# First channel block of a convolution taken in fp32 from the un-normalised input, the norm's factor applied to its sums

## The chip, the cores and the metric

The kernel runs on one core of one Trainium2 chip. The metric is the device time of one execution in microseconds (us). Three executions of the kernel before took 1934.17, 1934.20 and 1934.63 us, median 1934.2 us. A core has a matrix engine (TensorE, in the rows PE, its weight loads PEld), a vector engine (VectorE, DVE), a scalar engine (ScalarE, ACT), a general engine (GpSimd, POOL) and SyncE (SP), which here only issues DMAs. Each works through its own list of instructions in order.

## The reference

The model has two layers on 256 tokens of 2048 channels: a convolution module, an MLP, an attention layer, an MLP. The change touches only the start of the first one.

```python
def rms_norm(x, g):
    xf = x.astype(jnp.float32)
    y = xf * lax.rsqrt(jnp.mean(xf * xf, axis=-1, keepdims=True) + NORM_EPS)
    return (y * g.astype(jnp.float32)).astype(x.dtype)

def conv_module(h, w_pw1, b_pw1, w_dw, b_dw, ln_g, ln_b, w_pw2, b_pw2):
    u = h @ w_pw1 + b_pw1                     # 2048 -> 4096
    a, gate = jnp.split(u, 2, axis=-1)
    u = a * jax.nn.sigmoid(gate)
    u = lax.conv_general_dilated(...) + b_dw  # causal, depthwise, width 31
    u = jax.nn.silu(layer_norm(u, ln_g, ln_b))
    return u @ w_pw2 + b_pw2
...
h = rms_norm(x, norm_mixer_g[layer])
x = x + conv_module(h, ...)
```

## The kernel before

**Products in three parts.** A product of fp32 accuracy is made of three products in the rounded type fp32r: the operand is split into an upper part (`hi`, or the first half of the tile `xt`), rounded by ScalarE, and a remainder (`lo`), subtracted by VectorE or GpSimd. The sum of upper x upper, upper x lower and lower x upper is accumulated in PSUM (`conv_mm`, line 823). A weight half of 128x1024 numbers is rounded at L170 and its remainder made at L174.

**The convolution module.** The first matrix is worked in 16 channel blocks `c` of 128 channels. For each, two accumulators (`va` for the value, `ga` for the gate) take 16 slices `k` of 128 input channels. One block is 16 x 2 x 3 = 96 products of 128x256. The weights of a block come as two loads (`raw`, numbers 2c and 2c+1, two DMAs each, rows of 512 B), each split in two halves of four slices. `glu(c)` makes the gated value `ub` (padded, 256 tokens). Then VectorE adds the 31 taps of the depthwise convolution one instruction at a time (`add_tap`, L910) onto sums that ScalarE starts (`start_sum`, L880); a second sum of the same block ends in the tile `half`, GpSimd adds a side product to it, and L918 joins the two in `ca`. The order of the taps is written out by `dve_taps`: for block c it does most taps, and the last five come mixed with the first ones of block c+1.

**Order.** The whole stage stands under `tc.manual_schedule()`: each engine's order is the order of the code. While TensorE multiplies block c, VectorE adds the taps of block c-1, and ScalarE and GpSimd split the weights of blocks c and c+1.

**The start.** `x` is loaded in six pieces, the first 128 tokens on SP's queue (columns 0-1023, 1024-1535, 1536-2047), the other 128 on ACT's. TensorE turns x slice by slice (`turn0`, L1031) into PSUM, with extra transposes of the identity between (`busy`, L1001) that only keep it occupied. VectorE and ScalarE take sums of squares, and the factor 1/rms (`r0`) is turned into a row over the tokens and copied to `r_row` in the tile `b2`. Then `scaled` multiplies each slice in PSUM by the norm's gain and that row (L1075), `upper` rounds it into `xt` (L1090), `lower` takes the remainder (L1093), and block 0 is multiplied slice by slice as they come. Weight load 0 is asked for behind x on SP's queue. A DMA is issued only when the one eight before it has landed, since eight semaphores are used in turn.

Of the kernel before, what the change touches and what calls it, by code (L numbers as in the profile page):

```python
# [10 lines left out]
F32 = mybir.dt.float32  # L11
# [41 lines left out]
N_WARM = (10, 0, 16, 4)  # L53
# [26 lines left out]
def trunk_kernel(  # L80
# [677 lines left out]
    with ExitStack() as cx:  # L758
# [13 lines left out]
        xn = cv.tile([P, T, D], F32, tag="tok", name="xn")  # L772
        b2 = cv.tile([P, D], F32, name="b2")

        ca = cv.tile([P, KC, S], F32, tag="tok", name="ca")
        sh = cv.tile([P, KC, S], F32R, name="sh")
# [10 lines left out]
        raws, wjs = {}, {}  # L787


        def conv_load(n):  # L790
            if n < NU:
                c, k = n // UC, n % UC * 8
                raws[n] = load(
                    [rows(conv_w_pw1[0], k, 8, c * P, P), rows(conv_w_pw1[0], k, 8, D + c * P, P)], 8,
                    2 if n == 0 else 1,
                )
            elif n < NU + KC // 2:
                raws[n] = load([rows(conv_w_pw2[0], 2 * (n - NU), 2, 0, 2 * NB)], 2)
# [38 lines left out]
        def glu(c):  # L837
            ub = ubs[c] = branches[c % 3]
            sg = cv2.tile([P, S], F32, tag="sg", name=nm("sg"), bufs=1)
            va, ga = pss.pop(c)  # L840
            nc.scalar.activation(sg, ga[:, :S], AF.Sigmoid, bias=b_pw1[:, KC + c : KC + c + 1])
            if c in (0, KC - 2, KC - 1):
# [4 lines left out]
            else:  # L847
                vb = cv2.tile([P, S], F32, tag="vb", name=nm("vb"), bufs=1)
# [138 lines left out]
        for n in range(3):  # L987
            conv_load(n)
# [5 lines left out]
        with tc.manual_schedule():  # L994
# [17 lines left out]
            for i, (c0, c1) in enumerate(X_PARTS[1][:2]):  # L1012
                nc.scalar.activation(xn[:, 1, c0:c1], xs[:, 1, c0:c1], AF.Square, accum_out=xsq[:, i : i + 1])

# [3 lines left out]
            for n in range(NNB - 1):  # L1018
                block_stats(n)

            groups = [[0], [1]] + [[k, k + 1] for k in range(2, 10, 2)] + [[10], [11], [12, 13], [14, 15]]
            where, tiles = {}, {}

            def bank(pt, *ks):
                tiles[ks[0]] = pt
                for i, k in enumerate(ks):
                    where[k] = pt[:, i * S : (i + 1) * S]
# [5 lines left out]
            for k in range(2):  # L1033
                bank(acc_tile() if k else tr_tile(), k, k + 10)
            for k in range(2, 10, 2):
                bank(sum_tile() if k < 6 else sum2_tile() if k == 6 else acc_tile(), k, k + 1)
            for t in range(T):
                turn0(range(8), t)
                busy(N_WARM[t])

            early = [xn[:, 0, :S], b2[:, S : 2 * S]]
            nc.vector.tensor_copy(early[0], where[0])
            block_stats(NNB - 1)
            c0, c1 = X_PARTS[1][2]
            dve_squares(xn[:, 1, c0:c1], xs[:, 1, c0:c1], xsq[:, 2:3])
            for t in range(T):
                turn0(range(8, 11), t)
            pss[0] = [acc_tile()]
            busy(N_WARM[2])
# [9 lines left out]

            for t in range(T):  # L1060
                nc.tensor.transpose(
                    misc[:, t * P : (t + 1) * P], r0[:, t : t + 1].broadcast_to([P, P]), ident
                )
            r_row = b2[:, :S]
            conv_half(0, 0)
            nc.scalar.activation(early[1], where[1], AF.Copy)
            for t in range(T):
                turn0((11,), t)
            pss[0].append(acc_tile())
            for i in range(N_WARM[3]):  # L1070
                nc.tensor.transpose(pss[0][0][:, :P], ident, ident)

            def scaled(*ks):
                for k in ks:
                    nc.vector.scalar_tensor_tensor(  # L1075
# [868 lines left out]
```

## Time and profile before

| | |
|---|---|
| three runs | 1934.17, 1934.20, 1934.63 us (median 1934.2) |
| the profiled execution's own time | 1934.31 us, its span 1932.5 us |
| TensorE busy | 1921.0 us (99%), granted clock 0.999 |
| VectorE busy | 1592.2 us (82%) |
| ScalarE busy | 1095.6 us (57%) |
| GpSimd busy | 249.0 us (13%) |
| DMA | 375.50 MB, mean 194 GB/s |

The 1.8 us between the time and the span lie outside the first and last instruction. Busy time of an engine says how long it held instructions, not whether the kernel waited for it; that is read from the rows of idle time and from the chain of work that ended last. Times in rows are us from the start of the span unless marked ns. A row of the timeline gives start, length, engine, line, operation, the tile written, the tiles read, the count, and in brackets the idle time before it and what ended that. The conv stage before the second matrix is the first 210 us.

### The profile page before, as it was taken

The numbers are of one execution on the slowest core, as the hardware profiler recorded it, in microseconds if no ns is written. First come the engines' busy times: TensorE is split into PE (matmuls) and PEld (weight loads), VectorE is DVE, ScalarE is ACT, GpSimd is POOL, SyncE is SP. The second block draws the span as 40 slices with busy tenths as digits, with TensorE's granted clock in tenths as the row PEclk, the third lists the DMA queues.
The fourth block names the chain that finished last, engine by engine and source line by source line (L and its number), as shares of the span: only waits on it lengthen the run. The fifth ranks groups of instructions, "written<-read, shape, count | busy, mean of one in ns | idle before, by whom it ended". The sixth has DMA issues, their size and how long they took to land.

```text
span 1932.5 us, 28477 instructions
## 1 busy us (share of the span) xinstructions
PE 1921.0 (99%) x10725; PEld 1681.5 (87%) x10725; DVE 1592.2 (82%) x2457; ACT 1095.6 (57%) x1636; POOL 249.0 (13%) x208
## 2 busy tenths in 40 slices
PE   9999999999999999999999999999999999999998
PEld 8999888888888888888898998888888888888887
DVE  7999988877999776799976766877789987678998
ACT  5667755554555545555576655555555554455554
POOL 6999200000010100000001420000000010000000
PEclk9999999999999999999999999999999999999999
DMA  7766456665585866655656545465646776665774
GB/s 230 214 183 189 153 189 206 193 194 177 175 251 194 263 195 187 194 174 196 217 176 175 142 134 192 155 216 186 188 162 225 222 248 212 191 196 175 231 219 150
DMA packets 230427, 375.50 MB, mean 194 GB/s; under 512 B 16392, under 2 KB 107792, under 8 KB 230032
## 3 DMA queue, kind: packets, MB, share of 16 engines
q1 hardware_dynamic: 224640, 363.28, 58.7%
q0 software_dynamic: 4320, 7.87, 2.2%
q10 hardware_dynamic: 1328, 2.52, 0.4%
q8 instruction: 84, 1.38, 0.3%
q14 instruction: 55, 0.45, 0.1%
HBM read 363.68 MB, written 2.10 MB: 189 GB/s over the span
## 4 chain that ended last, share of the span: by engine, by line
PE 97%; DVE 2%; DMA 0%; ACT 0%; issue 0%; ACTq 0%; DVEq 0%
PE acc L655 24%; PE acc L205 15%; PE acc L203 15%; PE acc L204 15%; PE acc L656 13%; PE acc L823 8%; PE acc L1287 2%; DVE sum L910 1%; DMA xs<-in_x 0%; PE acc L1535 0%; PE acc L1566 0%; PE acc L1565 0%; PE acc L1536 0%; PE acc L1564 0%; PE acc L1537 0%; PE tr L267 0%
## 5 line engine op out<-in xcount | busy, mean ns | idle before, releaser
L174 DVE TENSOR_TENSOR lo<-raw,hi 128x1024 fp32r<-128x1024 f32 (+2 forms) x509 | 602.2, 1197 | 232.3 <-ACT hi L170 226.6
L170 ACT ACTIVATE hi<-raw 128x1024 fp32r<-128x1024 f32 (+2 forms) x574 | 583.9, 1036 | 361.1 <-PE acc L655 203.7
L655 PE MATMUL acc<-xt,hi 128*128 128x512 f32 x2048 | 710.6, 390 | 0.0
L656 PE MATMUL acc<-xt,lo 128*128 128x256 f32 x2048 | 577.5, 282 | 0.0
L655 PEld LDWEIGHTS acc<-xt,hi 128*128 128x128 f32 x2048 | 384.3, 188 | 80.7
L656 PEld LDWEIGHTS acc<-xt,lo 128*128 128x128 f32 x2048 | 387.1, 189 | 0.2
L497 ACT ACTIVATE hi<-raw 128x1024 fp32r<-128x1024 f32 x248 | 228.7, 948 | 228.3 <-DVE raw L505 134.0
L498 DVE TENSOR_TENSOR lo<-raw,hi 128x1024 fp32r<-128x1024 f32 x248 | 263.9, 1087 | 27.6 <-ACT hi L497 22.5
L203 PE MATMUL acc<-hi,sh 128*128 128x512 f32 x514 | 200.1, 389 | 0.0
L205 PE MATMUL acc<-lo,sh 128*128 128x512 f32 x514 | 200.1, 389 | 0.0
L203 PE MATMUL acc<-hi,gh 128*128 128x512 f32 (+1 forms) x516 | 200.0, 388 | 0.0
L205 PE MATMUL acc<-lo,gh 128*128 128x512 f32 (+1 forms) x516 | 199.9, 387 | 0.0
L204 PE MATMUL acc<-hi,gl 128*128 128x512 f32 (+1 forms) x516 | 199.9, 387 | 0.0
L823 PE MATMUL acc<-xt,hi 128*128 128x256 f32 x1024 | 180.2, 281 | 0.3 <-ACT b L1106 0.2
L204 PE MATMUL acc<-hi,sl 128*128 128x512 f32 x450 | 175.1, 389 | 0.0
L578 POOL DMA_DIRECT2D xs<-v x30 | 26.5, 994 | 1136.4 <-DVE lo L174 703.2
L910 DVE SCALAR_TENSOR_TENSOR sum<-ub,w_dw,sum 128x256 f32<-128x256 f32 x409 | 164.3, 481 | 3.6 <-ACT sum L880 3.0
L174 POOL TENSOR_TENSOR lo<-raw,hi 128x1024 fp32r<-128x1024 f32 x65 | 155.0, 2410 | 17.3 <-ACT hi L170 17.3
L823 PEld LDWEIGHTS acc<-xt,hi 128*128 128x128 f32 x1024 | 154.8, 188 | 1.1 <-ACT xt L1090 0.6
L823 PE MATMUL acc<-xt,lo 128*128 128x256 f32 x512 | 139.2, 279 | 0.0
L205 PEld LDWEIGHTS acc<-lo,sh 128*128 128x128 f32 x514 | 96.5, 188 | 20.4 <-DVE lo L498 0.3
L204 PEld LDWEIGHTS acc<-hi,gl 128*128 128x128 f32 x516 | 96.9, 188 | 19.9
(314 smaller groups left out, 2531.3 us busy)
## 6 DMA issues: line engine op xcount, KB each, us to landing
raw<-in_mlp_w SPq DMA_DIRECT2D x255, 1024.0 KB, 5.5
raw<-in_conv_w_pw SPq DMA_DIRECT2D x62, 512.0 KB, 5.1
raw<-in_conv_w_pw SPq DMA_DIRECT2D x16, 1024.0 KB, 5.1
raw<-in_mla_w_o SPq DMA_DIRECT2D x16, 1024.0 KB, 5.7
raw<-in_mla_w_kv_up SPq DMA_DIRECT2D x32, 256.0 KB, 3.9
xs<-v POOLq DMA_DIRECT2D x30, 256.0 KB, 7.8
raw<-in_mla_w_in SPq DMA_DIRECT2D x8, 576.0 KB, 3.8
raw<-in_mla_w_in SPq DMA_DIRECT2D x4, 1024.0 KB
```

The costliest lines, as they stand in the source:

```text
L170: nc.scalar.activation(hi, raw[:, js, :], AF.Copy)
L174: eng.tensor_tensor(lo, raw, hi.bitcast(F32), op=ALU.subtract)
L203: nc.tensor.matmul(ps, sh, mh, start=start, stop=False)
L204: nc.tensor.matmul(ps, sl, mh, start=False, stop=False)
L205: nc.tensor.matmul(ps, sh, ml, start=False, stop=stop)
L497: nc.scalar.activation(hi, src, AF.Copy)
L498: nc.vector.tensor_tensor(lo, src, hi.bitcast(F32), op=ALU.subtract)
L655: nc.tensor.matmul(ps[b], wh[:, bs], xhl(k), start=k == 0, stop=False)
L656: nc.tensor.matmul(ps[b][:, :S], wl[:, bs], xh(k), start=False, stop=k == KC - 1)
L823: nc.tensor.matmul(pss[c][b][:, :S], w[i][:, bs], (xh, xl)[j](k), start=k == i + j == 0, stop=end and k == k0 + nk - 1 and (i, j) == terms ...
L910: nc.vector.scalar_tensor_tensor(out=out, in0=ubs[c][:, w : w + S], scalar=tap(c, w), in1=base, op0=ALU.mult, op1=ALU.add)
L1287: nc.tensor.matmul(ps2[b][t], x_kt(k, t), w[:, bs], start=k == g == i == 0, stop=k == KC - 1 and i == len(group) - 1,)
```

## The change

Weight load 0 and x: SP's queue now carries the first two slices of weight load 0 (`first_load(0, 2)`, 256 KB) between the first and the second piece of x, and the rest of it behind x in two steps. `x_load(1, i)`, on ACT's queue, is as before.

Block 0: ScalarE (for three slices VectorE) copies each turned slice times the norm's gain from PSUM to an SBUF tile `xg` (`gained`). `first_products` multiplies the raw fp32 weights with `xg` as plain fp32 products: 32 products of 128x256 in the place of 96 in fp32r. No weight of block 0 is split. The factor 1/rms is multiplied into the two sums of block 0 in `glu(0)` by VectorE, since it depends on the token alone.

For blocks 1 to 15 the normed, split x is still needed: `scaled` multiplies pairs of slices of `xg` by `r_row`, `upper` and `lower` fill `xt` from SBUF, beside the products of block 0. The last two pairs, and the split of the first half of weight load 3, are put behind `glu(0)`. The extra transposes behind the second group of turns are gone. `xg` shares its place with `sh`, a tile of a later stage.

```diff
-N_WARM = (10, 0, 16, 4)
+N_WARM = 10
...
+        first_raw = wpool.tile([P, 8, 2 * P], F32, tag="raw", name=nm("raw"), bufs=3)
+        def first_load(j0, j1):
+            for b in range(2):
+                src = rows(conv_w_pw1[0], 0, 8, b * D, P)
+                nc.sync.dma_start(first_raw[:, j0:j1, b * P : (b + 1) * P], src[:, j0:j1, :])
...
         for i in range(3):
-            for t in range(T):
-                c0, c1 = X_PARTS[t][i]
-                (nc.sync, nc.scalar)[t].dma_start(xs[:, t, c0:c1], x[0, t * P : (t + 1) * P, c0:c1])
+            x_load(1, i)
+        x_load(0, 0)
+        first_load(0, 2)
+        x_load(0, 1)
+        x_load(0, 2)
+        first_load(2, 4)
+        first_load(4, 8)
...
             va, ga = pss.pop(c)
+            if c == 0:
+                vb = cv2.tile([P, S], F32, tag="vb", name=nm("vb"), bufs=1)
+                for o, ps in ((sg, ga), (vb, va)):
+                    nc.vector.tensor_tensor(o, ps[:, :S], b2[:, :S], op=ALU.mult)
+                va, ga = vb, sg
             nc.scalar.activation(sg, ga[:, :S], AF.Sigmoid, bias=b_pw1[:, KC + c : KC + c + 1])
-            if c in (0, KC - 2, KC - 1):
+            if c in (KC - 2, KC - 1):
...
+            def gained(k, eng=nc.scalar):
+                g = g_mix[0][:, k : k + 1]
+                if eng is nc.scalar:
+                    nc.scalar.activation(xg[:, k, :], where[k], AF.Copy, scale=g)
+                else:
+                    nc.vector.tensor_scalar(xg[:, k, :], where[k], scalar1=g, scalar2=None, op0=ALU.mult)
+            def first_products(*ks):
...
+                    nc.tensor.matmul(
+                        pss[0][b][:, :S], raws[k // 8][:, k % 8, b * P : (b + 1) * P], xg[:, k, :],
+                        start=k == 0, stop=k == KC - 1,
+                    )
...
+            def scaled(p):
+                row = r_row.rearrange("p (a n) -> p a n", a=1).broadcast_to([P, 2, S])
+                nc.vector.tensor_tensor(pair(xr, p), pair(xg, p), row, op=ALU.mult)
+            def upper(p):
+                nc.scalar.activation(part(p, 0), pair(xr, p), AF.Copy)
+            def lower(p):
+                nc.vector.tensor_tensor(part(p, 1), pair(xr, p), part(p, 0).bitcast(F32), op=ALU.subtract)
+            first_products(4, 5)
+            scaled(0)
+            upper(0)
+            for p in range(4):
+                for k in (8 + 2 * p, 9 + 2 * p):
+                    gained(k)
+                scaled(p + 1)
+                upper(p + 1)
+                lower(p)
+                first_products(6 + 2 * p, 7 + 2 * p)
...
+                if p in (1, 3):
+                    conv_half(2, p // 2)
...
+            first_products(14, 15)
+            lower(5)
...
                 glu(c - 1)
+                if c == 1:
+                    for p in (6, 7):
+                        scaled(p)
+                        upper(p)
+                    conv_half(3, 0)
+                    for p in (6, 7):
+                        lower(p)
```

**SP's queue at the start.** The head of it before, where `raw_129` is weight load 0:

```order
L771 DMA xs<-in_x 128x1024
L771 DMA xs<-in_x 128x512 x2
L160 DMA raw_129<-in_conv_w_pw 128x4x128 x4
L160 DMA raw_134<-in_conv_w_pw 128x8x128 x2
L160 DMA raw_137<-in_conv_w_pw 128x8x128 x2
```

and now, where `raw_110` is weight load 0 (the first of the two rows of x with 512 columns is columns 1024-1535):

```order
L778 DMA xs<-in_x 128x1024
L774 DMA raw_110<-in_conv_w_pw 128x2x128 x2
L778 DMA xs<-in_x 128x512 x2
L774 DMA raw_110<-in_conv_w_pw 128x2x128 x2
L774 DMA raw_110<-in_conv_w_pw 128x4x128 x2
L160 DMA raw_137<-in_conv_w_pw 128x8x128 x2
L160 DMA raw_140<-in_conv_w_pw 128x8x128 x2
```

Two small weight DMAs have moved ahead of two of the three pieces of x on this queue.

**TensorE from the wait for x to the first products.** Before (`acc_152<-ident` are the extra transposes, `y_238` is the norm's factor, the last rows are the first products):

```order
L1001 MATMUL acc_152<-ident 128x128 x16
L1061 MATMUL acc_152<-ident,y_238 128x128 x2
L1031 MATMUL acc_176<-ident,xs 128x128 x2
L1071 MATMUL acc_216<-ident 128x128 x4
L823 MATMUL acc_216<-xt_96,hi_249 128x256
L823 MATMUL acc_256<-xt_96,hi_249 128x256
```

Now (`acc_207` and `acc_208` are the two sums of block 0, `acc_205` to `sum_231` take the slices 8 to 15):

```order
L1048 MATMUL acc_205<-ident,xs 128x128 x2
L1048 MATMUL acc_206<-ident,xs 128x128 x2
L1064 MATMUL acc_207<-xg,raw_110 128x256
L1064 MATMUL acc_208<-xg,raw_110 128x256
L1064 MATMUL acc_207<-xg,raw_110 128x256
L1064 MATMUL acc_208<-xg,raw_110 128x256
L1048 MATMUL acc_205<-ident,xs 128x128 x2
L1048 MATMUL acc_206<-ident,xs 128x128 x2
L1048 MATMUL tr_230<-ident,xs 128x128 x2
L1048 MATMUL sum_231<-ident,xs 128x128 x2
L1064 MATMUL acc_207<-xg,raw_110 128x256
L1064 MATMUL acc_208<-xg,raw_110 128x256
```

The products no longer stand behind the norm's factor; the first of them stand behind four transposes of columns 1024-1535 of x.

**VectorE between block 0 and its first tap.** Before (`sum_437` and `tr_438` are the turned vectors and taps, L910 the first two taps):

```order
L1093 TENSOR_TENSOR xt_99<-sum_338,xt_99 128x2x256
L1142 COPY vecs<-sum_49_437 128x120
L1143 COPY w_dw<-tr_438 128x496
L844 SCALAR_TENSOR_TENSOR ub_121<-acc_216,vecs,sg_456 128x256
L910 SCALAR_TENSOR_TENSOR sum_461<-ub_121,w_dw,sum_461 128x256
L910 SCALAR_TENSOR_TENSOR sum_57_462<-ub_121,w_dw,sum_57_462 128x256
```

Now (L859 applies the factor to the sums, L1133 is `scaled`, L1139 `lower`, L931 the first two taps):

```order
L1139 TENSOR_TENSOR xt_98<-xn,xt_98 128x2x256 x2
L1165 COPY vecs<-sum_40_332 128x120
L1166 COPY w_dw<-tr_333 128x496
L859 TENSOR_TENSOR sg_352<-acc_208,b_125 128x256
L859 TENSOR_TENSOR vb_353<-acc_207,b_125 128x256
L1133 TENSOR_TENSOR xn<-xg,b_125 128x512 x2
L1139 TENSOR_TENSOR xt_99<-xn,xt_99 128x2x256 x2
L931 SCALAR_TENSOR_TENSOR sum_371<-ub_129,w_dw,sum_371 128x256
L931 SCALAR_TENSOR_TENSOR sum_51_372<-ub_129,w_dw,sum_51_372 128x256
```

Six instructions stand there for one; the product that makes `ub` has gone to GpSimd.

**GpSimd up to block 1's gated value.** Before (remainders of weight loads 0 to 4, then `ub_122` of block 1):

```order
L174 TENSOR_TENSOR lo_250<-raw_129,hi_249 128x1024
L174 TENSOR_TENSOR lo_275<-raw_129,hi_274 128x1024
L174 TENSOR_TENSOR lo_302<-raw_134,hi_301 128x1024
L174 TENSOR_TENSOR lo_348<-raw_134,hi_347 128x1024
L174 TENSOR_TENSOR lo_367<-raw_137,hi_366 128x1024
L174 TENSOR_TENSOR lo_396<-raw_137,hi_395 128x1024
L174 TENSOR_TENSOR lo_434<-raw_278,hi_433 128x1024
L174 TENSOR_TENSOR lo_468<-raw_278,hi_467 128x1024
L174 TENSOR_TENSOR lo_547<-raw_450,hi_546 128x1024
L174 TENSOR_TENSOR lo_551<-raw_450,hi_550 128x1024
L850 TENSOR_TENSOR ub_122<-vb_607,sg_605 128x256
```

Now (`raw_140`, `raw_289` and `raw_346` are weight loads 2, 3 and 4, `ub_129` and `ub_130` the gated values of blocks 0 and 1):

```order
L174 TENSOR_TENSOR lo_302<-raw_140,hi_301 128x1024
L174 TENSOR_TENSOR lo_324<-raw_140,hi_323 128x1024
L871 TENSOR_TENSOR ub_129<-vb_353,sg_352 128x256
L174 TENSOR_TENSOR lo_364<-raw_289,hi_363 128x1024
L174 TENSOR_TENSOR lo_378<-raw_289,hi_377 128x1024
L174 TENSOR_TENSOR lo_457<-raw_346,hi_456 128x1024
L174 TENSOR_TENSOR lo_461<-raw_346,hi_460 128x1024
L871 TENSOR_TENSOR ub_130<-vb_517,sg_515 128x256
```

The four remainders of block 0 are gone; the first half of weight load 3 stands behind block 0's gated value, where it stood ahead of it. Behind this place all engines have the same instructions in the same order as before, to the end of the program.

More of the change, by code (lines that the diff above doesn't have):

```diff
@@ L985, in ln_stats @@
                     nc.vector.bn_stats(out, cts[c][t][:, q * P : (q + 1) * P])
-        for n in range(3):
+        for n in range(1, 3):
             conv_load(n)
@@ L1066, in trunk_kernel @@
[L1066 to L1075, printed above, removed]
-                        out=where[k], in0=early[k] if k < 2 else where[k], scalar=g_mix[0][:, k : k + 1],
-                        in1=misc[:, :S] if k < 2 else r_row,
-                        op0=ALU.mult, op1=ALU.mult,
-                    )
@@ L1142, in trunk_kernel @@
+            scaled(5)
+            upper(5)
+            warm(AF.Sigmoid)
+            lower(4)
+            vt, wt = sum2_tile(), tr_tile()
+            turn(n_vecs2, vecs2_rows, vt)
+            for j in range(4):
+                nc.tensor.transpose(wt[:, j * NW : (j + 1) * NW], w_rows[j][:NW, :], ident[:NW, :NW])
+            first_products(14, 15)
+            lower(5)
             nc.vector.tensor_copy(vecs[:, n_vecs:], vt[:, :n_vecs2])
```

139 lines of the change are left out of this document (60 added, 79 removed).

## The prediction

> **What bounds the kernel now.** I read the page first, then a table by stretches, then the chain that ended last, then the timelines of single engines around the first block. The page and the table (busy time of each engine, then granted clock, DMA share, GB/s):
>
> ```profile
> span 1932.5 us, 28477 instructions
> PE 1921.0 (99%) x10725; PEld 1681.5 (87%) x10725; DVE 1592.2 (82%) x2457; ACT 1095.6 (57%) x1636; POOL 249.0 (13%) x208
> core 0: us, PE busy (x) PEld busy (x) DVE busy (x) ACT busy (x) POOL busy (x), PEclk, DMA share, GB/s
> 0.00:13.70 13.70, 11.08 (x68) 9.56 (x68) 6.16 (x21) 5.47 (x10) 2.17 (x12) 1.00 0.89 273
> 13.70:28.00 14.30, 14.03 (x114) 13.50 (x115) 12.17 (x28) 12.41 (x19) 13.66 (x7) 1.00 0.81 238
> 100.00:120.00 20.00, 20.00 (x174) 20.00 (x173) 19.91 (x52) 11.34 (x22) 19.28 (x11) 1.00 0.61 179
> ```
>
> TensorE is the bound of the program, so a microsecond saved on it early is saved at the end, unless another engine takes it back on the way. The third stretch says who could: in the conv stage VectorE (19.91 of 20) and GpSimd (19.28) are as full as TensorE. The chain, in order of time:
>
> ```profile
> 2.15 7.74 DMA xs<-in_x
> 12.29 0.45 PE acc L1061 x2
> 101.70 11.21 PE acc L823 x96
> 177.92 3.29 DVE sum L910 x9
> ```
>
> It runs through the landing of x, the norm's factor, then TensorE at 11.21 us for the 96 products of a block (0.117 each), and from 176 us through VectorE's taps. Both engines must come early for the stage to end early. The first block on TensorE:
>
> ```profile
> 9.77 1.91 PE L1001 MATMUL acc<-ident 128*128 128x128 f32 x16
> 13.72 0.38 PE L823 MATMUL acc<-xt,hi 128*128 128x256 f32 x1
> 26.61 0.59 PE L1138 MATMUL tr<-ident,stage 124*128 124x124 f32 x4
> 26.96 0.95 PE L823 MATMUL acc<-xt,hi 128*128 128x256 f32 x6
> ```
>
> Block 0 starts at 13.72; four of the last six products are its own, so block 1 starts at 26.96 + 4 x 0.117 = 27.43. That is what the change must beat.
>
> **The change part by part, on TensorE.** *The fp32 product.* The kernel has plain fp32 products of the same size in one other place:
>
> ```profile
> L873 PE MATMUL sum<-ub,dg x30: 377/378/483, 199.4 to 205.8; 128*128 128x256 f32 x30
> ```
>
> The code issues 15 there and the trace has 30 records, so a product is two. From first to last start 6.4 us / 29 = 0.221, or 0.441 us per product. 32 of them are 14.1 us, against 11.2 for the 96 they replace: the products by themselves cost 2.9 us more. Bounds: 0.378 (one record's length, if the second cost nothing) and 4 x 0.117 = 0.467; I take 0.441, the same form. The gain can only come from starting early.
>
> *The start.* The first products stand behind four transposes of columns 1024-1535 of x, the second piece on SP's queue; VectorE's statistics and the gain of slice 1 wait for it as well. Before, that piece is waited for until 7.53, the last piece until about 9.9:
>
> ```profile
> 7.53 0.69 DVE L1016 BATCH_NORM_STATS2 xst<-xs 128x6 f32<-128x512 f32 x1 [1.56 <-DMA xs<-in_x]
> 9.13 0.69 DVE L1016 BATCH_NORM_STATS2 xst<-xs 128x6 f32<-128x512 f32 x1 [0.43 <-DMA xs<-in_x]
> 9.92 0.42 DVE L229 SCALAR_TENSOR_TENSOR xn<-xs 128x256 f32<-128x256 f32 x1
> ```
>
> Now 256 KB of weights in rows of 512 B go ahead of it. How two queues share the DMA engines is in the packet counts, here of 5 to 7 us (q10 is ACT's queue with rows of 3 to 4 KB, q1 SP's with mostly 2 KB), and of 13 to 15 us, when only weights move:
>
> ```profile
> q10 hardware_dynamic: 84, 0.34, 62.0%
> q1 hardware_dynamic: 69, 0.11, 23.3%
> q1 hardware_dynamic: 1378, 0.69, 115.1%
> ```
>
> 84 packets against 69: turns by the packet, a packet being a row, whatever its length. Then 512 weight rows of 512 B alternate with ACT's 384 rows of x, and ACT's half of x is through before the weights are. Up to and with the second piece, 512 + 256 + 256 KB on SP and 1024 KB on ACT have moved, as much as all of x, which is there at 9.9 before. The other bound is a sharing by bytes: 7.53 + 0.26 MB at the 0.345 MB/us of the last row = 8.3. I take 9.7, close to the first, since VectorE was itself busy until 9.82.
>
> The Trainium skill ("DMA: Bandwidth & Descriptors", section Queues, rings and completion order) says that an engine goes round the queues by packets, but that a packet is typically 9 to 17 descriptors long. By that, 512 B rows would be served by the dozen and the piece would land near 8.3; the counts above, where a packet holds one row, speak against it.
>
> *The sum.* From 9.7: 16 transposes at 0.115 (the 16 of L1001 take 1.91) 1.84, products 14.1, two transposes of the factor 0.23, five of vectors and taps 0.5 (four of them start between 26.61 and 26.96 now). Together 16.7, so block 0 is through at 26.4, 1.0 earlier than 27.43. What must be there in time: weight load 0 with x is 3.15 MB, by 12.9 at 0.345 a microsecond from 9.9, needed for slice 4 at 15.3; load 1 by 16.0, needed at 18.8; load 2 by 19.0, and with rounding and remainder (1.05 and 2.41, below) by 23, needed at 26.4. The factor, at 12.2 in the chain and some 1.7 later now (last piece of x near 10.5 in place of 9.1, one gained slice ahead of it on VectorE), is ready near 14.0 for a place on TensorE near 15. Slices are gained on ScalarE in at most 0.48 each (128x256 out of PSUM, L849 below) ahead of their products. These cost nothing while the 14 us of products cover them; each is 1 us for 1 us once late.
>
> **VectorE, ScalarE and GpSimd at the seam behind block 0.** What stands there now:
>
> ```profile
> 27.99 0.48 DVE L844 SCALAR_TENSOR_TENSOR ub<-acc,vecs,sg 128x256 f32<-128x256 f32 x1
> 29.18 8.71 DVE L910 SCALAR_TENSOR_TENSOR sum<-ub,w_dw,sum 128x256 f32<-128x256 f32 x22 [0.71 <-ACT sum L880]
> 38.32 0.48 DVE L910 SCALAR_TENSOR_TENSOR sum<-ub,w_dw,sum 128x256 f32<-128x256 f32 x1
> 40.84 3.62 DVE L910 SCALAR_TENSOR_TENSOR sum<-ub,w_dw,sum 128x256 f32<-128x256 f32 x9 [2.03 <-ACT sum L880]
> 30.93 7.14 POOL L174 TENSOR_TENSOR lo<-raw,hi 128x1024 fp32r<-128x1024 f32 x3 [1.17 <-ACT hi L170]
> 39.46 0.74 POOL L850 TENSOR_TENSOR ub<-vb,sg 128x256 f32<-128x256 f32 x1 [1.39 <-ACT vb L849]
> 38.91 0.48 ACT L849 ACTIVATE vb<-acc,vecs 128x256 f32<-128x256 f32 x1 [0.86 <-PE acc L823]
> 40.23 0.57 ACT L880 ACTIVATE sum<-ub,vecs,w_dw 128x256 f32<-128x256 f32 x1
> 39.28 1.05 ACT L170 ACTIVATE hi<-raw 128x1024 fp32r<-128x1024 f32 x1
> 15.52 0.60 ACT L1090 ACTIVATE xt<-sum 128x512 fp32r<-128x512 f32 x1
> 8.28 0.42 DVE L1042 COPY xn<-tr 128x256 f32<-128x256 f32 x1
> 16.31 0.68 DVE L1093 TENSOR_TENSOR xt<-sum,xt 128x512 fp32r<-128x512 f32 x1
> L498 DVE TENSOR_TENSOR lo<-raw,hi 128x1024 fp32r<-128x1024 f32 x248 | 263.9, 1087 | 27.6 <-ACT hi L497 22.5
> 40.41 2.41 POOL L174 TENSOR_TENSOR lo<-raw,hi 128x1024 fp32r<-128x1024 f32 x1 [0.21 <-ACT hi L170]
> ```
>
> VectorE has 24 taps of block 0 from 29.18 to 38.7, then 2.0 us of idle time until block 1's sum; from there it never rests. The change puts onto this seam: two factor products (0.42 each, as the copy L1042), two `scaled` and two `lower` of 128x512 (0.54 to 0.68 each, half of L498 and the present L1093; the operation out of SBUF alone is nearer to L498), two `upper` (0.60) and one weight rounding (1.05) on ScalarE ahead of `start_sum`. In order from 26.6, when the last sum can be read: factor 27.05, `vb` on ScalarE 27.5, two `upper` 28.7, rounding 29.7, `start_sum` 30.2. The first tap is at 30.2 in place of 29.18, and the 24 end at 39.8. `scaled` and `lower` (2.5 us) lie beside ScalarE's work, and all of it inside the 2.0 us of rest: no loss by itself.
>
> GpSimd is nearer. It can take the first remainder of load 3 only from 29.7; four in a row at 2.37 end at 39.2. Only then comes block 1's gated value (0.74), then `start_sum` (0.57): VectorE goes on at about 40.6 against 40.84, while TensorE ends block 1 at 37.8 against 38.9. So GpSimd holds back 0.8 of the 1.0. Before, GpSimd had rested 1.39 there.
>
> VectorE wins most of that back. Its blocks alternate:
>
> ```profile
> 112.87 0.42 DVE L918 TENSOR_TENSOR ca<-sum,half 128x256 f32<-128x256 f32 x1
> 124.25 0.41 DVE L918 TENSOR_TENSOR ca<-sum,half 128x256 f32<-128x256 f32 x1
> 135.74 0.41 DVE L918 TENSOR_TENSOR ca<-sum,half 128x256 f32<-128x256 f32 x1
> ```
>
> 11.38 and 11.49 us, where TensorE takes 11.43 (two blocks of 11.21 and transposes). I read the longer one as a small wait for ScalarE's sum, behind TensorE. If TensorE leads, these 0.06 a block go, some 0.7 over the rest of the stage: VectorE then ends 0.25 + 0.7 = 0.95 earlier, TensorE 1.0. Behind the stage nothing moves, so about 1.0 reaches the end: 1934.31 - 1.0 = 1933.3 for the profiled execution, which lies 0.1 above the median: **1933.2**. A difference under 0.2% (3.9 us) is about what a measurement of this kernel can tell from no change.
>
> **The rivals.** *The queue shares by bytes.* The second piece at 8.3 and block 0 through at 25.0 to 25.5. GpSimd's row of remainders still decides, so VectorE gains about 1.0 at the seam and 0.7 later, and the end comes near 1932.4. For it: sharing need not be equal for rows of 512 B. Against: the counts.
>
> *The seam takes it all back, and more.* Place: block 1's gated value on GpSimd. If the four remainders start later than 30.7 (the `upper` pair waiting for `scaled`, or a late load 3), VectorE goes on later than 41.6, 0.75 after 40.84, and its slack is spent; every further microsecond is lost for good. With the second piece at 10.7 and 1 us more in the seam, VectorE goes on at 42.6: 1934.2 + 1.0 = 1935.2. For it: GpSimd at 19.28 of 20 has no room. Against: the sum above leaves 1.0 us.
>
> *TensorE slows down in the wait.* Without the fillers it stands from about 8.7 to 9.7. That it has a slow state is seen in the same six transposes early and late:
>
> ```profile
> 5.19 1.49 PE L1031 MATMUL sum<-ident,xs 128*128 128x128 f32 x6
> 8.19 0.82 PE L1031 MATMUL sum<-ident,xs 128*128 128x128 f32 x6
> ```
>
> The slow stretch lasts from 1.62 to about 6.5, though the clock column says 1.00. A second one of 4.9 us would lose half of it, 2.4: 1935.7; two, 1938.1. Against: the present kernel stands from 11.7 to 12.29 and again before 13.72, and stays fast. The Trainium skill ("TensorE: Matmul & The Clock Gate", Part 1) has the clock halved only after some 3.4 us without work, which by itself would rule this case out unless x comes far later.
>
> **How the numbers follow.** Forecast (1932.8 to 1933.9) 0.56; bytes 0.12; seam 0.20; slow TensorE 0.08; something unseen 0.04. No case reaches 1930.3, so faster by over 0.2% gets 0.03, from the unseen. Slower by over 0.2% (above 1938.1) needs two slow stretches or a seam some 3 us worse than priced: 0.07. Within: 0.90. The range runs from the byte case with a product at the cheap end (1931.4, TensorE 1 us better still but VectorE only partly) to the slow stretch (1935.8).
>
> **What would show it.** Right: the first product near 10.2, 0.44 apart, block 1's first product near 26.4, first taps near 30.2 and 40.6, GpSimd without rest between them. Wrong: block 1's start after 27.4; products waiting for weights or gained slices; products longer than 0.467; transposes at 0.2 us after 9; or an equal start of block 1's taps with a stage end that differs.

## The result and the profile after

The changed kernel takes 1937.26 us (median of 22 runs, 1935.46 to 1940.56) against 1934.34 (22 runs, 1933.92 to 1935.62) of the kernel before: 1.0016 times as long, 95% interval 1.0010 to 1.0023. That is 2.9 us slower, where 1.0 faster was forecast, and above the range (1931.4 to 1935.8). The profiled execution took 1938.44 us (4.1 more than the one of before), so its rows show more than the median loses.

The page's first line, and the chain's last pieces of TensorE in the conv stage (before, then after; start, length):

```profile
span 1936.7 us, 28367 instructions
```

```profile
170.28 5.62 PE acc L823 x48
```

```profile
174.28 5.62 PE acc L837 x48
```

All of the loss is there by the end of the conv stage: 174.28 - 170.28 = 4.0 us later, the spans 4.2. Where it arises is in the first 40 us. TensorE's timeline, first one row of before (the third product of block 1), then after (L1064 the fp32 products, two records each; L837 block 1):

```profile
27.74 0.28 PE L823 MATMUL acc<-xt,lo 128*128 128x256 f32 x1
```

```profile
9.73 1.89 PE L1064 MATMUL acc<-xg,raw 128*128 128x256 f32 x8
14.71 7.07 PE L1064 MATMUL acc<-xg,raw 128*128 128x256 f32 x32
22.45 1.99 PE L1064 MATMUL acc<-xg,raw 128*128 128x256 f32 x8 [0.66 <-ACT xg L1053]
27.06 0.59 PE L837 MATMUL acc<-xt,hi 128*128 128x256 f32 x2
27.48 0.28 PE L837 MATMUL acc<-xt,lo 128*128 128x256 f32 x1
32.74 0.27 PE L837 MATMUL acc<-xt,lo 128*128 128x256 f32 x1
33.32 0.51 PE L837 MATMUL acc<-xt,hi 128*128 128x256 f32 x2 [0.31 <-ACT hi L170]
35.76 0.39 PE L837 MATMUL acc<-xt,lo 128*128 128x256 f32 x1 [1.93 <-POOL lo L174]
```

The first products start at 9.73, and 16 of them take 7.07 (0.44 each). Block 1 starts at 27.06; its third product is at 27.48, where it was at 27.74, so the change is 0.26 us ahead there. At the half of block 1 TensorE stands for 0.31 + 1.93 us, for the first half of weight load 3. By the starts the stop costs more than these two idle times: from 32.74 to 35.76 three products take 3.02 us, where three take 0.35 elsewhere (0.117 each), so it costs 2.67. A table by stretches (busy time of each engine, granted clock, DMA share, GB/s) shows a second loss behind that wait, in the third column from the right:

```profile
36.00:37.00 1.00, 1.00 (x7) 1.00 (x7) 1.00 (x4) 1.00 (x2) 1.00 (x1) 0.57 0.39 117
37.00:38.00 1.00, 1.00 (x7) 1.00 (x7) 1.00 (x3) 0.39 (x1) 1.00 (x2) 0.50 0.00 0
38.00:39.00 1.00, 1.00 (x6) 1.00 (x6) 1.00 (x4) 0.00 (x0) 1.00 (x2) 0.50 0.00 0
39.00:40.00 1.00, 1.00 (x9) 1.00 (x8) 1.00 (x3) 0.00 (x0) 1.00 (x1) 0.72 0.29 83
```

Soon after it goes on, TensorE runs at half its clock: 6 or 7 matmuls per microsecond in place of 11. Now VectorE (L1139 the `lower` subtracts, L859 the first factor product), GpSimd (L174 the remainders) and ScalarE (L170 the roundings), whose rows say why load 3 was late:

```profile
19.21 0.69 DVE L1139 TENSOR_TENSOR xt<-xn,xt 128x512 fp32r<-128x512 f32 x1
23.31 1.71 DVE L1139 TENSOR_TENSOR xt<-xn,xt 128x512 fp32r<-128x512 f32 x1 [2.80 <-ACT xt L1136]
25.55 3.46 DVE L1139 TENSOR_TENSOR xt<-xn,xt 128x512 fp32r<-128x512 f32 x2
29.71 0.41 DVE L859 TENSOR_TENSOR sg<-acc,b 128x256 f32<-128x256 f32 x1
33.75 8.72 DVE L931 SCALAR_TENSOR_TENSOR sum<-ub,w_dw,sum 128x256 f32<-128x256 f32 x22 [0.35 <-ACT sum L901]
22.12 2.35 POOL L174 TENSOR_TENSOR lo<-raw,hi 128x1024 fp32r<-128x1024 f32 x1 [20.56 <-DMA stage<-in_conv_b_dw]
25.55 2.91 POOL L174 TENSOR_TENSOR lo<-raw,hi 128x1024 fp32r<-128x1024 f32 x1 [1.08 <-ACT hi L170]
33.34 9.39 POOL L174 TENSOR_TENSOR lo<-raw,hi 128x1024 fp32r<-128x1024 f32 x4 [1.09 <-ACT hi L170]
20.98 1.06 ACT L170 ACTIVATE hi<-raw 128x1024 fp32r<-128x1024 f32 x1 [1.80 <-DMA raw<-in_conv_w_pw]
32.22 1.05 ACT L170 ACTIVATE hi<-raw 128x1024 fp32r<-128x1024 f32 x1
```

With GpSimd idle a subtract takes 0.69. The one at 23.31 ends 0.55 behind the remainder that ran from 22.12 to 24.47; the two at 25.55 together end 0.55 behind the next remainder. Three subtracts take 1.71 + 3.46 = 5.17 us in place of 2.07. They are 3.1 us longer, and what stands behind them on VectorE comes late, the factor's products (29.71) and `scaled` 6 and 7; so do the `upper` parts on ScalarE, the rounding of load 3 in line behind those (32.22), and its remainder (33.34 to 35.7), which block 1 needs at 33.3. Part of the 3.1 us falls into rest that VectorE had: in the run without the remainders, below, the factor's product starts at 27.03 and the remainder of load 3 at 30.68, both 2.7 us earlier. The two load 2 remainders themselves start late, since load 2 landed at 20.98.

### The profile page after: what moved, and what is told of

It reads as the page before. It is cut to its first block, busy times and chain, and to the rows that moved or that the text cites. A ratio compares the mean times of both kernels' runs of the same rounds, so it can differ in the third digit from the quotient of the medians.

```text
span 1936.7 us, 28367 instructions
## 1 busy us (share of the span) xinstructions
PE 1921.3 (99%) x10673; PEld 1680.6 (87%) x10673; DVE 1593.7 (82%) x2450; ACT 1095.4 (57%) x1643; POOL 240.9 (12%) x205
## 4 chain that ended last, share of the span: by engine, by line
PE 96%; DVE 2%; DMA 1%; ACT 0%; issue 0%; SPq 0%; POOL 0%; ACTq 0%; DVEq 0%
PE acc L655 24%; PE acc L205 15%; PE acc L204 15%; PE acc L203 15%; PE acc L656 13%; PE acc L837 7%; PE acc L1317 2%; DVE sum L931 1%; PE acc L1565 0%; DMA raw<-in_conv_w_pw 0%; PE acc L1596 0%; PE acc L1595 0%; PE acc L1594 0%; PE acc L1566 0%; PE acc L1567 0%; DMA xs<-in_x 0%
## 5 line engine op out<-in xcount | busy, mean ns | idle before, releaser
L174 DVE TENSOR_TENSOR lo<-raw,hi 128x1024 fp32r<-128x1024 f32 (+2 forms) x509 | 602.0, 1197 | 231.5 <-ACT hi L170 224.7
L170 ACT ACTIVATE hi<-raw 128x1024 fp32r<-128x1024 f32 (+2 forms) x570 | 579.7, 1035 | 363.2 <-PE acc L655 203.0
L655 PEld LDWEIGHTS acc<-xt,hi 128*128 128x128 f32 x2048 | 384.5, 188 | 80.7
L498 DVE TENSOR_TENSOR lo<-raw,hi 128x1024 fp32r<-128x1024 f32 x248 | 263.9, 1087 | 29.4 <-ACT hi L497 25.2
L837 PE MATMUL acc<-xt,hi 128*128 128x256 f32 x960 | 171.7, 282 | 0.3 <-ACT hi L170 0.3
L578 POOL DMA_DIRECT2D xs<-v x30 | 26.4, 976 | 1137.7 <-DVE lo L174 703.3
L931 DVE SCALAR_TENSOR_TENSOR sum<-ub,w_dw,sum 128x256 f32<-128x256 f32 x409 | 164.1, 482 | 2.7 <-ACT sum L901 2.2
L174 POOL TENSOR_TENSOR lo<-raw,hi 128x1024 fp32r<-128x1024 f32 x61 | 145.8, 2410 | 27.3 <-DMA stage<-in_conv_b_dw 20.6
L837 PEld LDWEIGHTS acc<-xt,hi 128*128 128x128 f32 x960 | 147.4, 190 | 0.6 <-ACT hi L170 0.5
L837 PE MATMUL acc<-xt,lo 128*128 128x256 f32 x480 | 134.8, 281 | 1.9 <-POOL lo L174 1.9
L203 PEld LDWEIGHTS acc<-hi,gh 128*128 128x128 f32 x516 | 96.9, 188 | 19.9
```

The source lines that it names most:

```text
L170: nc.scalar.activation(hi, raw[:, js, :], AF.Copy)
L174: eng.tensor_tensor(lo, raw, hi.bitcast(F32), op=ALU.subtract)
L203: nc.tensor.matmul(ps, sh, mh, start=start, stop=False)
L498: nc.vector.tensor_tensor(lo, src, hi.bitcast(F32), op=ALU.subtract)
L655: nc.tensor.matmul(ps[b], wh[:, bs], xhl(k), start=k == 0, stop=False)
L837: nc.tensor.matmul(pss[c][b][:, :S], w[i][:, bs], (xh, xl)[j](k), start=k == i + j == 0, stop=end and k == k0 + nk - 1 and (i, j) == terms ...
```

## Experiments

My theory: a VectorE instruction with two SBUF operands and a GpSimd instruction do not run beside each other; the change put such instructions (its normed copies lie in SBUF, where those of the kernel before lay in PSUM) beside the remainders, and the delay reaches TensorE, where a wait costs its length and a stretch at half clock. Rivals: the order at the seam by itself, load 2's late landing, and two engines that are simply too full. Where not said otherwise an edit is made to the changed kernel. The kernel before took 1934.33 beside the first four runs, 1934.17 beside the next three, 1934.44 beside the last two.

**GpSimd's remainders of load 2 left out.**

```diff
-                wjs[n, h] = split_half(raws[n], h, nc.gpsimd if n <= NU else nc.vector)
+                if n == 2:
+                    hi = upper_half(raws[n], h)[0]
+                    wjs[n, h] = hi, hi
...
```

> The changed kernel with GpSimd's two remainders of load 2 left out (its rounded half stands in for its remainder), so nothing runs on GpSimd between 22 and 29 us. If VectorE's two-input subtracts were lengthened by GpSimd (1.71 and 2.68 us in place of 0.69), all eight now take 0.69, the vectors' copy starts near 27 in place of 28.93, load 3's first remainder ends near 34 in place of 35.7, TensorE waits 0.7 us or less for it, and the time comes to 1935.0 to 1935.5. If their length has another cause, they stay over 1.5 us and the time stays at 1937.0 or above.

1933.48 us (11 runs, 1932.96 to 1935.6), ratio 0.9997 (0.9988 to 1.0005). VectorE and GpSimd (L1143 the subtracts, of which the middle one, at 24.19, takes 0.69 too; L863 the first factor product):

```profile
22.94 0.69 DVE L1143 TENSOR_TENSOR xt<-xn,xt 128x512 fp32r<-128x512 f32 x1 [1.98 <-ACT xt L1140]
25.65 0.69 DVE L1143 TENSOR_TENSOR xt<-xn,xt 128x512 fp32r<-128x512 f32 x1 [0.77 <-ACT xt L1140]
27.03 0.41 DVE L863 TENSOR_TENSOR sg<-acc,b 128x256 f32<-128x256 f32 x1
30.68 9.51 POOL L174 TENSOR_TENSOR lo<-raw,hi 128x1024 fp32r<-128x1024 f32 x4 [1.10 <-ACT hi L170]
```

All subtracts are back at 0.69. Load 3's remainder ends at 33.10 and the product that needs it starts at 33.14: just in time. The gain, 3.8 us, is larger than the 1.8 to 2.3 that I expected: I had the wait shrink, and it vanished. Load 2 landed nearly as late here (its rounding starts at 20.60), and the stage ends at 170.10, 0.2 before that of the kernel before, so its late landing alone doesn't make the loss. The profiled execution itself took 1935.6 us, the longest of the 11: it lost 1.5 us behind the stage, where both kernels have the same instructions, for a reason that I don't know.

**Load 3's first half rounded before the gated value.**

```diff
-                glu(c - 1)
                 if c == 1:
+                    conv_half(3, 0)
+                glu(c - 1)
+                if c == 1:
                     for p in (6, 7):
                         scaled(p)
                         upper(p)
-                    conv_half(3, 0)
```

> The changed kernel with the rounding and remainder of load 3's first half put ahead of block 0's gated value and of the two late upper parts. If the order at the seam is the cause, the rounding starts at 28.5 to 29.5 in place of 32.22, the remainder ends by 32.5 (block 1 needs it at 33.3), TensorE waits for nothing there, its clock stays at 1.00, block 1 starts at 27.06 as now, and the time comes to 1933.6 to 1934.6, with no more scatter than the kernel before. If the loss lies in what came earlier (late weights, lengthened subtracts), the time stays at 1936.5 or above.

1938.21 us (1936.57 to 1940.35), ratio 1.0021 (1.0011 to 1.0030): a miss. VectorE, GpSimd and ScalarE:

```profile
24.37 3.44 DVE L1139 TENSOR_TENSOR xt<-xn,xt 128x512 fp32r<-128x512 f32 x2
29.17 3.49 DVE L1133 TENSOR_TENSOR xn<-xg,b 128x512 f32<-128x512 f32 x2
28.56 2.40 POOL L174 TENSOR_TENSOR lo<-raw,hi 128x1024 fp32r<-128x1024 f32 x1 [1.90 <-ACT hi L170]
35.65 7.03 POOL L174 TENSOR_TENSOR lo<-raw,hi 128x1024 fp32r<-128x1024 f32 x3 [3.53 <-ACT hi L170]
19.63 1.06 ACT L170 ACTIVATE hi<-raw 128x1024 fp32r<-128x1024 f32 x1
```

The remainder is early as expected (28.56), and now it meets `scaled` 6 and 7 (L1133, also two SBUF operands): 3.49 for two in place of 1.28. The second half of load 3 is what comes late (35.65). Load 2 was in time in this execution (19.63, no wait), and the subtracts were as slow: its landing isn't the cause either. TensorE waits 0.9 and 1.9 us, and its clock halves behind that.

**TensorE kept busy in the wait.**

```diff
+                if c == 1:
+                    keep_warm(ident, 22)
                 conv_mm(c, 8)
```

> The changed kernel with 22 transposes of the identity (about 2.4 us) put on TensorE where it waits for load 3's first remainder. The wait is as long as before, but TensorE is not idle in it. If the half clock at 36 to 39.6 us follows from the idle stretch, the clock now stays at 1.00 and the time comes 1.2 to 1.9 us under the changed kernel's in the same runs (1935.4 to 1936.0). If it has another cause, the dip stays, and the time is the changed kernel's or above it (1937.2 or more).

1936.24 us (1935.74 to 1939.43), ratio 1.0012 (1.0004 to 1.0021), 1.0 under the changed kernel and just above the interval that I gave. The time alone doesn't settle it, since the changed kernel's ratio (1.0010 to 1.0023) overlaps with this one; the rows do. The chain of waits, after and then this run (start, length; the 190 products behind the wait):

```profile
35.76 24.00 PE acc L837 x190
```

```profile
32.02 2.40 PE acc L250 x22
34.67 22.45 PE acc L837 x190
```

The same products take 24.00 behind an idle TensorE and 22.45 behind a busy one, with the clock column at 1.00 from 20 to 46 us in this run. So the half clock follows from the idle stretch, and the two together make the cost: in the changed kernel 2.24 of idle time (2.67 by the starts) and 1.55 of clock.

**A probe in the kernel before.** Into its VectorE row, beside GpSimd's remainders:

```diff
+            junk = cv.tile([P, NB], F32, name="junk")
...
                 lower(g[i])
+                if i == 2:
+                    for _ in range(3):
+                        nc.vector.tensor_tensor(junk, xs[:, 0, :NB], xs[:, 0, NB : 2 * NB], op=ALU.subtract)
+                        nc.vector.tensor_scalar(junk, xs[:, 0, :NB], scalar1=2.0, scalar2=None, op0=ALU.mult)
```

> The kernel before with six extra VectorE instructions of 128x512 fp32 put in turn, near 16.8 us, beside GpSimd's row of remainders: three subtracts of two SBUF tiles, three products of one SBUF tile by a constant. If a VectorE instruction with two SBUF inputs waits for GpSimd's whole instruction, each subtract takes 1.2 to 3 us, or a GpSimd remainder beside it grows above 2.4 us, and the products by a constant take 0.4 to 0.7. If not, subtracts take 0.69 and GpSimd stays at 2.37 each.

One run, 1942.18 us. VectorE and GpSimd:

```profile
17.54 1.57 DVE L1128 TENSOR_TENSOR junk<-xs 128x512 f32<-128x512 f32 x1
19.15 2.46 DVE L1129 TENSOR_SCALAR junk<-xs 128x512 f32<-128x512 f32 x1
21.65 0.69 DVE L1128 TENSOR_TENSOR junk<-xs 128x512 f32<-128x512 f32 x1
22.37 0.43 DVE L1129 TENSOR_SCALAR junk<-xs 128x512 f32<-128x512 f32 x1
16.17 5.16 POOL L174 TENSOR_TENSOR lo<-raw,hi 128x1024 fp32r<-128x1024 f32 x2 [0.64 <-ACT hi L170]
```

GpSimd works until 21.33, and up to there the subtract takes 1.57; behind it 0.69. The product by a constant, which I had taken for harmless, took 2.46 beside GpSimd and 0.43 without it. The second remainder is lengthened in turn: the two take 5.16, where two take 4.73 elsewhere. The kernel before thus has the meeting too, once such instructions are put in; its own subtracts read PSUM.

**The three subtracts' operand kept in PSUM.** No instruction changes its place in the order; the normed copies of pairs 3 to 5 are written into the PSUM banks in which their slices were turned:

```diff
+            def turned(p):
+                if p in (3, 4, 5):
+                    return tiles[p].rearrange("p (a n) -> p a n", n=S)
+                return pair(xr, p)
...
-                nc.vector.tensor_tensor(pair(xr, p), pair(xg, p), row, op=ALU.mult)
+                nc.vector.tensor_tensor(turned(p), pair(xg, p), row, op=ALU.mult)
...
-                nc.scalar.activation(part(p, 0), pair(xr, p), AF.Copy)
+                nc.scalar.activation(part(p, 0), turned(p), AF.Copy)
...
-                nc.vector.tensor_tensor(part(p, 1), pair(xr, p), part(p, 0).bitcast(F32), op=ALU.subtract)
+                nc.vector.tensor_tensor(part(p, 1), turned(p), part(p, 0).bitcast(F32), op=ALU.subtract)
```

> The changed kernel in its own order, with the three normed copies whose subtracts met GpSimd (channel pairs 3, 4 and 5) kept in the PSUM banks that their channels were turned in, so that their subtracts read one operand from SBUF in place of two; GpSimd's remainders stay. If two SBUF inputs are what makes VectorE wait for GpSimd, these three subtracts take 0.69 us each beside the remainders, and the time is near that of the run without remainders: 1933.4 to 1934.6. If GpSimd slows any VectorE instruction beside it, the subtracts stay at 1.5 us or more and the time at 1936.5 or above.

1933.26 us (11 runs, 1933.15 to 1934.48), ratio 0.9995 (0.9987 to 1.0004), just under the interval that I gave. VectorE (L1138 `scaled`, L1144 the subtracts), GpSimd, and the chain's piece at the stage's end:

```profile
22.09 0.69 DVE L1144 TENSOR_TENSOR xt<-sum,xt 128x512 fp32r<-128x512 f32 x1 [0.86 <-ACT xt L1141]
22.70 1.31 DVE L1138 TENSOR_TENSOR acc<-xg,b 128x512 f32<-128x512 f32 x1
23.93 1.52 DVE L1144 TENSOR_TENSOR xt<-acc,xt 128x512 fp32r<-128x512 f32 x2
20.93 2.52 POOL L174 TENSOR_TENSOR lo<-raw,hi 128x1024 fp32r<-128x1024 f32 x1 [19.36 <-ACT hi L170]
24.30 2.35 POOL L174 TENSOR_TENSOR lo<-raw,hi 128x1024 fp32r<-128x1024 f32 x1 [0.85 <-ACT hi L170]
169.28 5.62 PE acc L837 x48
```

Beside the same remainders the subtracts take 0.69 each (the 1.52 of the last row of two holds 0.15 between them), while `scaled` 5, which still has two SBUF operands, waits for the end of the first remainder (1.31). TensorE waits for none of it, and the stage ends 5.0 us before the changed kernel's and 1.0 before the kernel before. Of the kernels that leave nothing out it is the fastest: 0.9 under the kernel before by the medians, and 9 of its 11 runs lie below the lowest of the other's 27 (1933.86), though the interval still holds 1. The profiled execution was the longest of the 11 (1934.48): it was 1.0 ahead at the end of the stage and lost 1.2 behind it, so its own total doesn't show the gain.

**Load 2's roundings behind the last slices.**

```diff
-                if p in (1, 3):
-                    conv_half(2, p // 2)
             scaled(5)
             upper(5)
+            conv_split(2)
```

> The changed kernel with both roundings of load 2 (and so its remainders on GpSimd) put behind the last gained slices and upper parts on ScalarE. The subtracts of pairs 3 to 5 then run before GpSimd starts (near 23 us): 0.69 us each; block 1 still starts near 27.06, since the turn of the vectors' rows waits for their DMA; load 3's first remainder ends near 33.3, when it is needed. If the place of the two instructions against each other is what counts, the time is 1933.5 to 1935.0. If it is instead the late landing of load 2 itself that costs, its later rounding makes TensorE wait for load 2's remainder and the time stays at 1936.5 or above.

1936.3 us (1935.51 to 1937.69), ratio 1.0011 (1.0002 to 1.0020). The subtracts are quick, and the meeting has moved:

```profile
21.85 1.43 DVE L1139 TENSOR_TENSOR xt<-xn,xt 128x512 fp32r<-128x512 f32 x2
26.29 3.73 DVE L1133 TENSOR_TENSOR xn<-xg,b 128x512 f32<-128x512 f32 x2
23.59 4.73 POOL L174 TENSOR_TENSOR lo<-raw,hi 128x1024 fp32r<-128x1024 f32 x2 [22.02 <-ACT hi L170]
```

`scaled` 6 and 7 now run into the second remainder and into the gated value behind it on GpSimd (28.26 to 29.47), and TensorE waits 1.9 us as before, with the half clock behind it (23.92 us for the 190 products). Block 1 started at 25.56, 1.5 us earlier than I expected, and that didn't help. My expectation had looked at the subtracts alone: a VectorE that is early only meets GpSimd with its next instruction of the kind.

**Vectors and taps over GpSimd's queue, besides.** On top of that edit:

```diff
-            vecs2_rows = stage_rows(cv, vec_rows2, nc.sync)
...
+        vecs2_rows = stage_rows(cv, vec_rows2, nc.gpsimd)
         w_rows = []
...
-            nc.sync.dma_start(w_rows[i][:NW, :], taps)
+            nc.gpsimd.dma_start(w_rows[i][:NW, :], taps)
```

> As the run with load 2's roundings behind the slices, and the rows of the vectors and taps fetched over GpSimd's queue at the start in place of SP's, where they stand ahead of load 3. SP then issues load 3 near 17.5 to 19 us in place of 23.28, and the vectors' turn waits for nothing. If block 1's start and load 3's landing are what is left to gain at the seam, block 1 starts near 25.3 in place of 27.06, TensorE waits for nothing behind it, and the time is 1931.8 to 1933.0, under the kernel before. If the end of the stage is set elsewhere (VectorE's taps, or the small transfers colliding with x at the start), it is 1934 or above.

1936.18 us (1935.48 to 1937.46), ratio 1.0010 (1.0001 to 1.0019): no gain. SP issued load 3 at 18.91 and 19.32, and it had landed by 24.64, but ScalarE rounded it only at 30.99 (30.59 in the run before this), behind the `upper` parts that waited for `scaled` 6 and 7: these took 3.71 us at 26.71. So load 3's landing was not what was late.

**The late `scaled` moved up.** Again on top of load 2's roundings behind the slices:

```diff
             scaled(5)
             upper(5)
+            scaled(6)
+            scaled(7)
...
                     for p in (6, 7):
-                        scaled(p)
                         upper(p)
```

> As the run with load 2's roundings behind the slices, and the two late products by the factor (channel pairs 6 and 7) moved up too, behind that of pair 5, where GpSimd is still idle; they took 3.73 us beside the remainders at the seam. If that meeting was all that was left of the loss there, they take 0.69 each, the upper parts 6 and 7 follow the gated value at once, load 3's first remainder starts near 29 in place of 31.71 and ends near 31.6, TensorE waits 0.3 us or less for it with its clock at 1.00, and the time is 1932.2 to 1933.8, under the kernel before. If VectorE and GpSimd are simply too full at the seam, the wait only moves to the subtracts 6 and 7 and to the gated value, and the time is 1935 or above.

1935.01 us (1934.04 to 1935.65), ratio 1.0002 (0.9993 to 1.0011). VectorE's timeline and TensorE's waits:

```profile
21.25 1.89 DVE L1133 TENSOR_TENSOR xn<-xg,b 128x512 f32<-128x512 f32 x3
27.51 3.13 DVE L1139 TENSOR_TENSOR xt<-xn,xt 128x512 fp32r<-128x512 f32 x2 [1.10 <-ACT xt L1136]
```

```profile
PE acc L837 <- POOL lo L174: 0.9, 2, 0.5
```

Each `scaled` out of GpSimd's way is quick again, and 1.3 us come back. The two subtracts that are left at the seam are lengthened in their turn; TensorE waits twice 0.5, and its clock column stays at 1.00. By its time and by where the wait went this is my second case, at its edge. Still, two engines that are too full are not the reason: with the operand in PSUM both had the same work to do, and the time was 1933.26.

**Shorter instructions on GpSimd.** The changed kernel's order, the remainders of load 2 in four pieces each:

```diff
+                if n == 2:
+                    hi, lo, raw = upper_half(raws[n], h)
+                    for q in range(4):
+                        lower_half(hi[:, q : q + 1, :], lo[:, q : q + 1, :], raw[:, q : q + 1, :], nc.gpsimd)
+                    wjs[n, h] = hi, lo
...
```

> The changed kernel in its own order, with each of load 2's two remainders on GpSimd cut into four instructions of 128x256 (0.74 us each by the nearest row, so 3.0 in place of 2.4 for the four). If VectorE waits for the end of GpSimd's running instruction, the three subtracts that met it take at most 0.69 + 0.74 = 1.4 us each in place of 1.71 and 2.68, and the time falls to 1934.5 to 1936.3. If VectorE is instead held as long as GpSimd has work in its queue, or the two share a port at a slower rate, the subtracts take as long as now or longer (2 us or more) and the time stays at 1937 or above.

1936.76 us (1935.27 to 1938.13), ratio 1.0011 (1.0002 to 1.0020). VectorE (L1145 the subtracts, L1139 `scaled`) and GpSimd:

```profile
22.10 0.93 DVE L1145 TENSOR_TENSOR xt<-xn,xt 128x512 fp32r<-128x512 f32 x1 [0.90 <-ACT xt L1142]
24.09 2.36 DVE L1145 TENSOR_TENSOR xt<-xn,xt 128x512 fp32r<-128x512 f32 x2
27.80 2.34 DVE L1139 TENSOR_TENSOR xn<-xg,b 128x512 f32<-128x512 f32 x2
20.90 7.54 POOL L174 TENSOR_TENSOR lo<-raw,hi 128x256 fp32r<-128x256 f32 x8 [19.34 <-DMA stage<-in_conv_b_dw]
```

The subtracts take 0.93 and, the last two, 1.2 each, under the bound of 1.4: VectorE is held for the running instruction and no longer. The time did not fall as expected (0.5 under the changed kernel, which is within the noise): GpSimd's row is longer (until 28.44), so it meets `scaled` 6 and 7 at the seam, and TensorE still waits 1.9.

The Trainium skill ("SBUF — State Buffer", section "SBUF: two separate sides") says that VectorE and GpSimd share one pair of SBUF ports as an exclusive lock: a VectorE operation with two SBUF inputs (against a GpSimd operation that reads SBUF) or in a two-port mode takes it for the whole instruction, and whoever comes later is blocked. All of these runs agree: 0.69 against 1.71 with two SBUF operands, 0.69 with one in PSUM, 1.2 behind quarter-length instructions, and the product by a constant, 0.43 or 2.46, would be the two-port mode, though no row here names the mode. I had not weighed this section.

## Why the prediction was wrong

- *The fp32 product, 0.441 us*: right; 16 in 7.07 us.
- *The start at 9.7*: right; the second piece of x was there at 9.21 and the first product ran at 9.73, and in the profiled executions of the other kernels made from the changed one the piece came at 9.4 to 9.95.
- *Block 0 through at 26.4, with weights and slices hidden under the products*: the cover had gaps. Load 2, expected at 19.0, landed at 20.98 in the profiled execution, and its rounding stands ahead of slices 12 and 13 in ScalarE's row, so TensorE stood 0.66 us; block 1 started at 27.06. Where load 2 was in time (19.63 in the run with load 3's rounding first) it started at 25.99. This step moved the start by up to 1 us but not the sign, as the run without remainders shows.
- ***VectorE free for the factor at 26.6*** ("In order from 26.6 ... factor 27.05"): this is the step that failed. The seam's sum prices `scaled` and `lower` of pairs 6 and 7 alone, 2.5 us for the four, and they took 1.28 + 1.59 = 2.9. The subtracts of pairs 3 to 5 ahead of them got no term at all: they were taken as covered by the products of block 0. Beside load 2's remainders they took 5.17 in place of 2.07, and the factor's first product started at 29.71. In the run without remainders it started at 27.03 and was through at 27.44, near the forecast; with the operand in PSUM it started at 26.13.
- *The price of 0.54 to 0.68*: both rows behind it come from places without this meeting. L498 stands where GpSimd has no remainders, and L1093 has an operand in PSUM. The lower end is also a misreading: the 1087 ns of L498 are a mean over two forms, and kept apart they are 1221 ns for 128x1024 and 684 for 128x512. So 0.68 was the price for VectorE alone (0.69 measured), and the price beside a remainder was missing.
- *"No loss by itself", load 3's rounding through at 29.7*: fell with it. ScalarE rounded from 32.22 to 33.27, the four remainders started at 33.34 in place of 29.7, the first tap at 33.75 in place of 30.2. What made this costly is a time that the prediction did not work out: when TensorE needs the first remainder of load 3. By its own figures that is 26.4 + 48 x 0.117 = 32.0, and the remainder was to end at 29.7 + 2.37 = 32.1. There was no margin, so VectorE's delay became a stop of TensorE.
- *The rival "the seam takes it all back, and more"*, with its point of decision at 30.7 for the four remainders: this is the case that came, at a chance of 0.20. Its condition, `upper` waiting for `scaled`, was met, though for a reason that it doesn't name. Its price (1935.2) was too low, and its place half right: not only block 1's gated value was late, TensorE itself ran out of weights.
- *The rival of a slow TensorE*: a slow stretch came, but at 36 us and not in the wait for x, and it cost 1.55 us. By the table the clock lost 0.43 + 0.50 + 0.50 + 0.28 = 1.71 us, a slow stretch of 3.4 us. The four other profiled executions in which TensorE waited 1.9 us in one piece (load 3 rounded first, load 2's roundings behind, GpSimd's queue, quarters) lost 1.70 or 1.71 us of clock too. I let the Trainium skill ("TensorE: Matmul & The Clock Gate", Part 1) argue against this rival: it has the clock halved after an idle window of about 3.4 us. Here 1.9 us without products were enough, so the measurement decides. For the way back the section names about 3.4 us of sustained work, and the 3.4 us here agree.
- *A small reading*: "two blocks of 11.21 and transposes" for 11.43 should be one block of 11.21 and two transposes (0.22).

The sum by rows, for the profiled execution: block 1 is 0.26 ahead (27.48 against 27.74), the stop takes 2.67, the half clock 1.55: 3.96 of the 4.0 at the stage's end. That the changed kernel's runs spread over 5.1 us, where those with the operand in PSUM spread over 1.3, fits a wait and a half clock of which every execution gets its own share; that was not tried by itself.

## What to carry to other kernels

Before a value moves from PSUM to SBUF, look at what GpSimd does at that moment: a VectorE instruction that read one operand from SBUF and now reads two is no longer priced by its own row alone: what is left of GpSimd's running instruction comes on top (here up to 2.0 us on 0.69). Moving such a pair apart in the order only helps if nothing else of the kind comes to stand there; an operand left in PSUM settles it at once. Work out, too, when TensorE needs what stands at the end of such a row. And a wait on TensorE near 2 us was followed by the half clock in all five executions that had one, so it is to be priced with it.

## What was not expected of the hardware

- A 128x512 fp32 product by a constant on VectorE, SBUF to SBUF, takes 0.43 us alone and took 2.46 beside GpSimd's remainders: one tensor operand is enough for the meeting.
- The remainder is lengthened too when VectorE comes first: 2.91 us in place of 2.35.
- TensorE's clock fell to 0.50 behind 0.31 and 1.93 us without products, and stayed at 1.00 behind two waits of 0.5, and with 22 transposes in the gap. In the probe, where TensorE stood for 5.69 us, the clock fell while it still stood (from about 22.2 us, the next product at 25.56) and came back at about 29.1, after 6.8 us, twice the 3.4 of the others.
